# An elementwise product and GELU on one core: y's 5 KB rows loaded and computed first, its 59 KB rows loaded as 44 and 15 KB

## The chip, the cores and the metric

The kernel runs on one core of one Trainium2 chip. The metric is the device time of one execution in microseconds (us). Three runs of the kernel before took 119.72, 119.79 and 119.82 us; their median, 119.79 us, is the time before.

## The reference

x and y are float32 arrays of 1024 x 4096. The output has the same shape and type:

```python
z = x * y
return (0.5 * z * (1 + np.tanh(np.sqrt(2 / np.pi) * (z + 0.044715 * z ** 3)))).astype(np.float32)
```

So the kernel reads 2 x 16.78 MB, multiplies elementwise, applies GELU in its tanh form, and writes 16.78 MB.

## The kernel before

As the work is elementwise, the kernel takes x, y and the output as flat arrays and cuts them in three pieces (`PIECES`). Piece (a, b) is 128 x (b - a) numbers in one run of memory, seen as 128 rows, one for each partition of SBUF. In columns of 4 bytes the pieces are 0 to 1280 (rows of 5 KB, 640 KB in all), 1280 to 17664 (rows of 64 KB, 8192 KB) and 17664 to 32768 (rows of 59 KB, 7552 KB). A transfer of a piece has 128 rows, which the trace shows as 128 data packets, 8 for each of the 16 DMA engines, and 16 packets of 4 bytes that close it.

All of x has its place in SBUF (`xs`, 128 x 32768). The product and the GELU are written over x in place, and the stores read from there. y goes through a smaller buffer (`ys`, 128 x 20440), so that a part of y can be loaded only when the products that read the older part in its place are done. `Y_LOADS` lists the loads of y in order, each with its columns and its place in `ys`; `Y_FREE` says how many products must be done before each; `STEPS` cuts each load into the widths that DVE multiplies at a time; `STORES` lists the stores in order. Everything has its own semaphore (`sem_x`, `sem_y` and `sem_o` by transfer, `sem_mul` and `sem_act` as counts of products and GELUs).

The order on each engine is the order in which the code issues. There is no scheduler.

- SP issues nearly all transfers, into one queue. Its order before: x's 5 KB rows (hoisted to the start of the program, line 71), then a wait until these have landed, y's 64 KB rows (line 75), x's 59 KB rows (line 71), y's 59 KB rows after the third product, y's 5 KB rows after the fourth product. Then the stores (line 115): the 64 KB rows once the last but one load of y has landed (line 113) and their GELUs are done (line 114), the 59 KB rows and the 5 KB rows once their GELUs are done. At the end SP waits for the stores and clears the semaphores.
- ACT issues one transfer, x's 64 KB rows, hoisted to the start as well, into a queue of its own. Then it does one GELU for each product (line 106), after that product (line 105).
- DVE waits for the load of x and of y that a stretch needs (lines 94 and 95) and multiplies (line 98): four products of 4096 columns, seven of 2048 and one of 768, and one of 1280.

Of the kernel before, what the change touches and what calls it, by code (L numbers as in the profile page):

```python
# [1 line left out]

# [4 lines left out]


F32 = mybir.dt.float32
GELU = mybir.ActivationFunctionType.Gelu_apprx_tanh  # L10

PIECES = [(0, 1280), (1280, 17664), (17664, 32768)]

Y_LOADS = [(1280, 17664, 4056), (17664, 32768, 0), (0, 1280, 15104)]

Y_FREE = [0, 3, 4]

STEPS = [[4096] * 4, [2048] * 7 + [768], [1280]]  # L20
STORES = [(1280, 17664), (17664, 32768), (0, 1280)]
Y_BUF = 20440


def _hoist(nc, issued):

    here = nc.cur_bb.bb.instructions
    first = nc.main_func.blocks[0].instructions
    for ins in issued:
        del here[next(k for k, i in enumerate(here) if i is ins or i.name == ins.name)]  # L30
    engine = issued[0].engine
    at = next(
        k
        for k, i in enumerate(first)
        if i.engine == engine and type(i).__name__ == "InstDrain"
    )
    first[at:at] = issued


@with_exitstack  # L40
def kernel(
    ctx: ExitStack,
    tc: tile.TileContext,
    x: bass.AP,
    y: bass.AP,
    out: bass.AP,
):
    nc = tc.nc
    P = nc.NUM_PARTITIONS

    def columns(t, a, b):

        flat = t.flatten_outer_dims().rearrange("r c -> (r c)")
        pa, pb = next(q for q in PIECES if q[0] <= a and b <= q[1])
        return flat[P * pa : P * pb].rearrange("(p c) -> p c", p=P)[:, a - pa : b - pa]


    tc.close()
    tc.compile()  # L59

    xs = nc.alloc_sbuf_tensor("xs", [P, PIECES[-1][1]], F32).ap()
    ys = nc.alloc_sbuf_tensor("ys", [P, Y_BUF], F32).ap()
    sem_x = [nc.alloc_semaphore(f"sem_x{i}") for i in range(len(PIECES))]
    sem_y = [nc.alloc_semaphore(f"sem_y{i}") for i in range(len(Y_LOADS))]
    sem_mul = nc.alloc_semaphore("sem_mul")
    sem_act = nc.alloc_semaphore("sem_act")
    sem_o = [nc.alloc_semaphore(f"sem_o{i}") for i in range(len(STORES))]

    def load_x(i, engine=nc.sync):
        a, b = PIECES[i]  # L70
        return engine.dma_start(out=xs[:, a:b], in_=columns(x, a, b)).then_inc(sem_x[i], 16)

    def load_y(i):
        a, b, r = Y_LOADS[i]
        return nc.sync.dma_start(
            out=ys[:, r : r + b - a], in_=columns(y, a, b)
        ).then_inc(sem_y[i], 16)

    _hoist(nc, [load_x(0).ins])
    _hoist(nc, [load_x(1, nc.scalar).ins])  # L80
    nc.sync.wait_ge(sem_x[0], 16)
    load_y(0)
    load_x(2)
    for i in range(1, len(Y_LOADS)):
        if Y_FREE[i]:
            nc.sync.wait_ge(sem_mul, Y_FREE[i])
        load_y(i)

    n = 0
    done = {}  # L90
    for i, (a, b, r) in enumerate(Y_LOADS):
        for j, (xa, xb) in enumerate(PIECES):
            if xa <= a < xb:
                nc.vector.wait_ge(sem_x[j], 16)
        nc.vector.wait_ge(sem_y[i], 16)  # L95
        c = a
        for w in STEPS[i]:
            nc.vector.tensor_mul(  # L98
                out=xs[:, c : c + w],
                in0=xs[:, c : c + w],  # L100
                in1=ys[:, r + c - a : r + c - a + w],
            ).then_inc(sem_mul, 1)
            n += 1
            done[c + w] = n
            nc.scalar.wait_ge(sem_mul, n)
            nc.scalar.activation(  # L106
                out=xs[:, c : c + w], in_=xs[:, c : c + w], func=GELU
            ).then_inc(sem_act, 1)
            c += w

    for i, (a, b) in enumerate(STORES):
        if i == 0:
            nc.sync.wait_ge(sem_y[-2], 16)
        nc.sync.wait_ge(sem_act, done[b])
        nc.sync.dma_start(out=columns(out, a, b), in_=xs[:, a:b]).then_inc(sem_o[i], 16)
    for i in range(len(STORES) - 1):
        nc.sync.wait_ge(sem_o[i], 16)
    nums = sorted(s.num for s in [*sem_x, *sem_y, *sem_o[:-1], sem_mul, sem_act])
    assert nums == list(range(nums[0], nums[-1] + 1))
    nc.sync.sem_clear(range(nums[0], nums[-1] + 1))  # L120
    nc.sync.wait_ge(sem_o[-1], 16).then_inc(sem_o[-1], -16)


# [1 line left out]
_INS = ['x', 'y']  # L125
_OUTS = [((1024, 4096), 'float32')]


# [23 lines left out]
```

## Time and profile before

| what | value |
|---|---|
| median of the runs | 119.79 us |
| span of the profiled execution, first to last instruction | 118.5 us |
| its own time | not listed apart from the span; the median of the runs is 1.27 us above the span |
| bytes moved | 50.33 MB, 425 GB/s over the span |
| DVE busy | 35.2 us in 13 products |
| ACT busy | 31.0 us: 13 GELUs and the load of a table |
| y's 64 KB rows | issued at 13.57, landed at 42.56 us |
| y's 59 KB rows | issued at 55.78, landed at 78.25 us |
| y's 5 KB rows | issued at 60.1, landed at 79.8 us |
| stores | issued from 78.27 to 97.7 us, last closing packets at 118.5 us |

Means of one product and one GELU by shape, in ns: 4419 and 3616 for 4096 columns, 2285 and 1910 for 2048, 1481 and 1252 for 1280, 950 and 826 for 768.

How to read it: the span runs from the first to the last instruction of the profiled execution. "Busy" of DVE and ACT is the time in their instructions; an issue of a transfer is not counted as busy, and its data move later, on the 16 DMA engines. "Landed" is the moment when the semaphore of a transfer is complete. The chain of waits is followed back from the last instruction of the compute engines. The packet records of the trace give start, duration, size and queue of each packet, though not the DMA engine that moved it.

### The profile page before, as it was taken

How to read it: one execution, taken by the hardware profiler on the slowest of the kernel's cores; microseconds unless marked ns; L12 is line 12 of the kernel's file. 1: busy time of each engine (PE TensorE's matmuls, PEld its weight loads, DVE VectorE, ACT ScalarE, POOL GpSimd, SP SyncE). 2: the span in 40 equal slices, each digit the busy share in tenths (PEclk: the TensorE clock that was granted, in tenths of full speed). 3: DMA queues.
4: the chain of work that ended last, by engine and by line, in shares of the span. 5: the costliest groups of instructions: out<-in, count | busy, mean ns of one | idle time of the engine just before them, and what ended most of it. 6: DMA issues, size and time to landing. Idle time of an engine off the chain costs nothing.

```text
span 118.5 us, 82 instructions
## 1 busy us (share of the span) xinstructions
DVE 35.2 (30%) x13; ACT 31.0 (26%) x14; POOL 0.2 (0%) x4
## 2 busy tenths in 40 slices
DVE  0000000000000069999920000059999940000000
ACT  4000000000000000977975000006998990000000
POOL 0000000000000000000000000000000000000000
DMA  9888899889988897797797797798899887977975
GB/s 492 382 382 382 354 575 487 354 354 398 664 354 354 354 652 326 326 652 326 326 632 347 326 632 347 326 575 354 354 531 531 354 354 326 652 326 326 652 326 221
DMA packets 1296, 50.33 MB, mean 425 GB/s; under 512 B 144, under 2 KB 144, under 8 KB 528
## 3 DMA queue, kind: packets, MB, share of 16 engines
q1 hardware_dynamic: 1152, 41.94, 82.2%
q10 hardware_dynamic: 144, 8.39, 16.5%
HBM read 33.55 MB, written 16.78 MB: 425 GB/s over the span
## 4 chain that ended last, share of the span: by engine, by line
DMA 55%; DVE 24%; ACT 3%; issue 1%; DVEq 0%
DMA ys<-in_y_dram 43%; DVE xs L98 24%; DMA xs<-in_x_dram 11%; ACT xs L106 3%; DVEq L95 0%
## 5 line engine op out<-in xcount | busy, mean ns | idle before, releaser
L98 DVE TENSOR_TENSOR xs<-xs,ys 128x2048 f32<-128x2048 f32 (+3 forms) x13 | 35.2, 2777 | 60.9 <-DMA ys<-in_y_dram 60.9
L106 ACT ACTIVATE xs<-xs 128x2048 f32<-128x2048 f32 (+3 forms) x13 | 29.7, 2301 | 65.1 <-DVE xs L98 65.1
L106 ACT ACT_TABLE_LOAD x1 | 1.3, 1283 | 1.6 <-PEq L59 1.6
L136 POOL MEMSET const-bfloat16-1.0<- 128x1 bf16 x1 | 0.1, 103 | 0.0
L136 POOL MEMSET const-uint8-127<- 128x1 uint8 x1 | 0.1, 102 | 0.0
L136 POOL MEMSET const-float32-0.0<- 128x1 f32 x1 | 0.1, 100 | 0.2 <-issue 0.2
L136 POOL MEMSET const-float32-1.0<- 128x1 f32 x1 | 0.1, 99 | 0.0
## 6 DMA issues: line engine op xcount, KB each, us to landing
xs<-in_x_dram SPq DMA_DIRECT2D x1, 7552.0 KB, 46.5
ys<-in_y_dram SPq DMA_DIRECT2D x1, 7552.0 KB, 22.5
out_dram<-xs SPq DMA_DIRECT2D x1, 7552.0 KB, 20.4
xs<-in_x_dram SPq DMA_DIRECT2D x1, 640.0 KB, 13.6
ys<-in_y_dram SPq DMA_DIRECT2D x1, 640.0 KB, 19.7
out_dram<-xs SPq DMA_DIRECT2D x1, 640.0 KB, 20.8
xs<-in_x_dram ACTq DMA_DIRECT2D x1, 30.4
ys<-in_y_dram SPq DMA_DIRECT2D x1, 29.0
```

The source lines that it names most:

```text
L98: nc.vector.tensor_mul(out=xs[:, c : c + w], in0=xs[:, c : c + w], in1=ys[:, r + c - a : r + c - a + w],).then_inc(sem_mul, 1)
L106: nc.scalar.activation(out=xs[:, c : c + w], in_=xs[:, c : c + w], func=GELU).then_inc(sem_act, 1)
L136: nc = _bacc.Bacc("TRN2", target_bir_lowering=False, num_devices=1)
```

## The change

y's 5 KB rows become the first of y's loads. SP issues them directly behind the program's start, without the wait for x's 5 KB rows, and y's 64 KB rows and x's 59 KB rows behind them. The product and GELU of the 5 KB stretch come first on DVE and ACT. y's 59 KB rows are loaded as two transfers, 44 KB and 15 KB of each row: the 44 KB after the third product, the 15 KB after the fourth. As the 5 KB product now counts as the first, these are the second and third product of the 64 KB stretch. The products of the 59 KB stretch are cut accordingly: five of 2048 and one of 1024, then 2048 and 1792. There are still 13 products and 13 GELUs. The order of the stores stays; line 113 (`sem_y[-2]`), which is unchanged, now names the 44 KB load where it named the 59 KB load.

```diff
-Y_LOADS = [(1280, 17664, 4056), (17664, 32768, 0), (0, 1280, 15104)]
+Y_LOADS = [(0, 1280, 0), (1280, 17664, 4056), (17664, 28928, 0), (28928, 32768, 11264)]
 
-Y_FREE = [0, 3, 4]
+Y_FREE = [0, 0, 3, 4]
 
-STEPS = [[4096] * 4, [2048] * 7 + [768], [1280]]
+STEPS = [[1280], [4096] * 4, [2048] * 5 + [1024], [2048, 1792]]
 STORES = [(1280, 17664), (17664, 32768), (0, 1280)]
 Y_BUF = 20440
...
     _hoist(nc, [load_x(0).ins])
     _hoist(nc, [load_x(1, nc.scalar).ins])
-    nc.sync.wait_ge(sem_x[0], 16)
     load_y(0)
+    load_y(1)
     load_x(2)
-    for i in range(1, len(Y_LOADS)):
+    for i in range(2, len(Y_LOADS)):
         if Y_FREE[i]:
             nc.sync.wait_ge(sem_mul, Y_FREE[i])
         load_y(i)
```

## The prediction, made before the changed kernel was run

> **What bounds the kernel now.** I read four views, in this order: the chain of work that ended last, the busy times by stretch, the waits of the DMA queue's own engine (SP), and the DMA issues. The chain in order of time says that every long step before the tail is a load:
>
> ```profile
> 0.00 13.55 DMA xs<-in_x_dram
> ...
> 13.57 28.99 DMA ys<-in_y_dram
> ...
> 55.78 22.47 DMA ys<-in_y_dram
> ...
> 78.35 1.53 DVE xs L98
> ...
> 93.88 3.80 ACT xs L106 x3
> ```
>
> The chain stops at ACT's last GELU at 97.7 us, yet the span is 118.5 us: the last 21 us are stores, which the chain leaves out. So I go by stretches that cover it all (columns: length, DVE, ACT and POOL busy, clock, mean busy share of the 16 DMA engines, GB/s):
>
> ```profile
> 0.00:1.00 1.00, 0.00 (x0) 0.00 (x0) 0.20 (x4) 1.00 0.00 0
> 1.00:42.60 41.60, 0.00 (x0) 1.28 (x1) 0.00 (x0) 1.00 1.03 442
> 42.60:60.40 17.80, 17.43 (x4) 11.13 (x4) 0.00 (x0) 1.00 1.00 434
> 60.40:78.30 17.90, 0.00 (x0) 3.34 (x1) 0.00 (x0) 1.00 0.92 399
> 78.30:79.90 1.60, 1.55 (x1) 0.00 (x0) 0.00 (x0) 1.00 1.97 835
> 79.90:99.20 19.30, 16.22 (x9) 15.26 (x9) 0.00 (x0) 1.00 1.00 430
> 99.20:117.00 17.80, 0.00 (x0) 0.00 (x0) 0.00 (x0) 1.00 0.92 395
> 117.00:118.50 1.50, 0.00 (x0) 0.00 (x0) 0.00 (x0) 1.00 0.63 256
> ```
>
> A transfer is booked in the stretch where its packet starts, so a stretch can show more than 1 and its neighbour less (0.92 beside 1.97); together they are full. The reader is to see that no stretch between 1 us and 118 us has idle DMA engines, while DVE and ACT are idle most of the time. The packet records of the trace say it exactly: from the first packet (1.01 us) to the last (118.12 us) 16 packets run at every moment, but for 1 to 2 us (13.0 of 16, the ramp) and 79 to 80 us (14.8 of 16). The bound is the bytes: 50.33 MB through 16 busy engines. A change can win only the small holes, or lose by adding packets or opening a hole.
>
> SP's waits show which holes could be there:
>
> ```profile
> SPq L75 <- DVE xs L98: 45.4, 2, 41.4
> SPq L117 <- DMA out_dram<-xs: 18.9, 1, 18.9
> SPq L115 <- ACT xs L106: 18.7, 2, 17.9
> SPq L115 <- DMA ys<-in_y_dram: 14.5, 1, 14.5
> SPq L75 <- DMA xs<-in_x_dram: 12.0, 1, 12.0
> ```
>
> The last line is the wait that the change removes, the fourth the one that it moves to another transfer. Both are idle time of an issuing engine; each costs something only if the queue runs dry behind it.
>
> **The base.** The trace has only the span of the profiled execution, 118.5 us; the median of the runs, 119.79 us, is 1.27 us above it. Nothing in the change touches what lies around the span, so I add differences to 119.79.
>
> **Part 1: the wait for x's first piece goes, y's 5 KB rows go second in SP's queue.** The wait held SP until 13.57 us. Meanwhile x's first 64 KB piece, issued by ACT, kept all 16 engines busy (16.0 of 16 running in each microsecond from 2 to 15 us). So the wait cost nothing and its removal gains 0. The 5 KB packets of y now alternate with x's 64 KB packets as x's own 5 KB packets did. What does a pair cost? In the records from 10 to 13 us, where the two kinds alternate, every 5 KB packet takes its usual 196 ns and every 64 KB packet 2418 ns: 0 extra. From 5 to 10 us, 23 such pairs show 31.5 ns of extra time per engine in all, or 22 ns a pair (31.5 x 16 / 23). In the first round (2.3 to 5.2 us) x's 64 KB packets take 124 ns more than 2420 on the mean. Upper bound: 8 pairs per engine at 124 ns, 0.99 us; lower bound 0, as nothing in the rows makes packets shorter. I take 0, since y's 5 KB packets alternate later, where the 10 to 13 us row is nearest.
>
> **Part 2: what is then late.** All of y's 64 KB stretch comes 8 packets later, 8 x 196 ns = 1.57 us: it lands at 42.56 + 1.57 = 44.1 us. DVE's four products (4.43 us the first, 4.33 the others) end at 48.6, 53.0, 57.3 and 61.7 us. The product of the 5 KB stretch is long done by then: its 8 packets alternate with x's 64 KB ones, which end by about 23 us, so it lands near 25 us, and its 1.48 us on DVE and 1.25 us on ACT lie under y's load. SP's two later y loads wait for the third and fourth product, as before by number; with the 5 KB product counted, that is now 53.0 and 57.3 us. The queue then still holds x's last piece, until 60.41 + 1.57 - 0.42 = 61.6 us (0.42 is from the last packet's end to the landing: 77.83 and 78.25 us for y's 59 KB load). So SP has 8.6 and 4.3 us in hand, and the queue doesn't run dry. Were it late, each microsecond past 61 us would cost one.
>
> **Part 3: y's 59 KB rows as 44 and 15.** One transfer more. Packets of 5 KB take 196 ns and of 59 KB 2232 ns: 37.7 ns per KB and 7.5 ns per packet. So 44 KB takes 1666 ns, 15 KB 573 ns, together 7.5 ns over 2232. Eight rows per engine: 0.06 us; one more 4-byte closing packet, 9 ns. Sum +0.07 us. Records in one queue abut (the next starts within 4 ns), so no other cost is seen; the bounds are 0.01 us (closing packet alone) and 0.10 us (with such a 4 ns at each of the 8 packets added).
>
> The Trainium skill, "DMA: Bandwidth & Descriptors", section "Anatomy of one DMA", fits each DMA (on GpSimd's path) as about 2.0 us fixed plus its bytes; a transfer more would by that make 119.79 + 2.0 = 121.8 us, an estimate from that page. The trace has a row against it: y's 640 KB landed 1.57 us after the 59 KB load before it (79.82 and 78.25 us), exactly its packets' time, so that behind another transfer no fixed part is left.
>
> **Part 4: the first store's cover.** The first store is issued once the last but one y load has landed. Now that leaves 1.57 us of y's 5 KB packets to hide it: issue 78.27 us, its first packets 79.11 to 79.39 us. Engines that had ended earlier (from 78.9 us) stood idle, 1.2 us over 16 engines, 0.08 us on the mean; the engine that ended last (79.38 us) went on at 79.39 us without a hole. After: 44 KB land at 60.41 + 1.57 + 8 x 1.666 = 75.3 us, the store is issued then and 8 x 573 ns = 4.6 us of packets cover it. The hole closes. Gain: 0 if the last engine sets the end, 0.08 us if the engines even out. Their spread falls from 0.27 us at 79 us to 0.17 us at the end, so they do in part; I take 0.04 us.
>
> **Part 5: the end.** The 44 KB products start at 75.4 us: five of 2048 columns (2.3, then 2.2 us each) and 1024 (1.1 us, between 0.87 for 768 and 1.40 for 1280) end at 87.6 us, 2048 and 1792 at 91.8 us, ACT's last at 93.5 us. The 15 KB rows have landed at 75.3 + 4.6 = 79.9 us. So the second store is issued at 93.5 instead of 96.5 us, the last right behind it instead of at 97.7 us, both still ahead of the first store's end (98.9 us). That was covered before as well: gain 0. The last store has the same 5 KB rows: 0.
>
> **Sum:** 0 + 0.07 - 0.04 + 0 = +0.03 us, so **119.82 us**.
>
> **Rivals.** (a) *Faster: the hole at 79 us is larger without the profiler.* The last engine's first store packet comes 1.12 us after the issue (79.39 - 78.27), the others' 0.84 us and more. x's first 64 KB load needed 2.17 us (issue 0.13, first packet 2.30 us). With that the last engine would stand 1.05 us, and closing it gives 119.79 - 1.05 + 0.07 = 118.81 us. It decides where the last engine's delay is over 1.43 us (0.31 us of hole). Against it: the profile shows no hole on that engine. Chance 0.09. (b) *Slower: the opening's mixed packets hold each other up.* Place: 3 to 24 us, 8 pairs per engine. At the first round's 124 ns a pair: 119.82 + 0.99 = 120.8 us; it decides from about 26 ns a pair. For it: the first round, and 22 ns from 5 to 10 us (0.18 us, 120.0 us, just inside the bound). Against it: 0 from 10 to 13 us. Chance 0.08. (c) *The change doesn't close the hole*, because the store is held by ACT or the 15 KB rows are late: 119.79 + 0.07 = 119.86 us. ACT is done with the stretch at 65 us, ten before it is needed. It lies within the forecast's bound; its chance is in the remainder.
>
> **Numbers.** About 0.2% (0.24 us) is what a measurement of this kernel tells from no change. Within it: forecast and (c), 0.83; faster 0.09; slower 0.08. The forecast's own bounds are -0.08 + 0.01 and +0.10, so 119.72 to 119.89; the runs shown differ by 0.1 us; with 22 ns a pair it is 120.0, and toward (a) I go as far as a store whose first packets come after 1.01 us, as those of x's first load did: 0.17 us later, 119.79 - 0.17 + 0.01 = 119.63 us. With a few hundredths for the runs' spread on both sides the range is 119.60 to 120.02 us; the rest of (a) and (b), 0.17, lies outside.
>
> **What would show it.** Right: 16 engines full from 3 to 118 us; no hole near 79 us; y's 64 KB landing near 44.1 us, first store issued near 75.3 and last near 93.9 us; span within 0.15 us of 118.5. Wrong: 64 KB packets over 2440 ns in the opening (b), a span much shorter than its packets' sum allows (a), or y's later loads issued after 61 us, which would open a hole that I have not priced in.

## The result, and the profile after

The changed kernel takes **121.14 us** (median of five runs, 120.77 to 121.28) against 119.79 us before (five runs, 119.72 to 119.90): 1.0099 times the time, 95% interval 1.0088 to 1.0110. It is slower by 1.35 us, where 0.03 us was forecast. The profiled execution took 120.77 us, with a span of 119.4 us; before, the span was 118.5 us.

The chain of waits of the changed kernel, in order of time (start, length, what):

```profile
1.95 42.14 DMA ys<-in_y_dram
...
52.98 22.30 DMA ys<-in_y_dram
...
75.37 5.35 DVE xs L98 x3
...
91.77 1.70 ACT xs L106
```

Up to 75 us all went as worked out. y's 64 KB rows landed at 44.10 us (forecast 44.1), the next load was issued at 52.98 us (53.0), the 44 KB rows landed at 75.27 us (75.3). ACT ends at 93.5 us (93.5), four microseconds earlier than before, and the whole is still later. As before, the chain says nothing of the end, since it stops at ACT.

The waits of SP (us in total, times, longest) show the two that the change moved:

```profile
SPq L75 <- DVE xs L98: 54.1, 2, 50.1
SPq L117 <- DMA out_dram<-xs: 23.0, 1, 23.0
SPq L115 <- ACT xs L106: 17.8, 1, 17.8
SPq L115 <- DMA ys<-in_y_dram: 10.0, 1, 10.0
```

The wait for x is gone. The first store's wait for y (last line) is shorter, 10.0 instead of 14.5 us, as that store now needs only the 44 KB rows. But SP stands 4.1 us longer at the end, waiting for stores (line 117). The stores are issued earlier and don't end earlier.

Where the time went is in five stretches of 1 us around the turn from loads to stores (DVE, ACT and POOL busy, clock, DMA share, GB/s; a packet is booked where it starts):

```profile
76.00:77.00 1.00, 1.00 (x1) 0.00 (x0) 0.00 (x0) 1.00 1.02 430
77.00:78.00 1.00, 1.00 (x2) 0.31 (x1) 0.00 (x0) 1.00 1.05 307
78.00:79.00 1.00, 1.00 (x1) 1.00 (x1) 0.00 (x0) 1.00 1.02 215
79.00:80.00 1.00, 1.00 (x2) 0.71 (x2) 0.00 (x0) 1.00 1.33 508
80.00:81.00 1.00, 1.00 (x1) 1.00 (x1) 0.00 (x0) 1.00 1.82 786
```

The DMA share stays at 1 and the rate falls to half: 215 GB/s from 78 to 79 us. The engines are busy and move less. The packet records name the victims. Of the 128 packets of 15 KB, 48 took over 590 ns (up to 1342), the others 573 to 581; the sum above 573 is 1.02 us per engine, between 76.5 and 80.4 us. (The first expectation below says 58 packets, a miscount, and 0.98 us, which is the sum above 581 ns.) The store's first packet comes at 79.7 us, though it was issued here:

```profile
75.29 0.35 SPq L115 DMA_DIRECT2D out_dram<-xs  x1
```

From the first packet to the last the changed kernel needs 118.03 us, before 117.11 (1.01 to 118.12 us; the 118.5 us that the table before calls the last closing packets is the moment when their semaphore is complete): 0.92 us more. The slow packets (1.02), one transfer more (0.07) and the closed hole (-0.08) make 1.01 us, against these 0.92. The profiled execution is the fastest of the five; what the median has on top of it, 0.37 us, is in no trace.

### The profile page after: what moved, and what is told of

It reads as the page before. It is cut to its first block, busy times and chain, and to the rows that moved or that the text cites. A ratio compares the mean times of both kernels' runs of the same rounds, so it can differ in the third digit from the quotient of the medians.

```text
span 119.4 us, 84 instructions
## 1 busy us (share of the span) xinstructions
DVE 35.3 (30%) x13; ACT 31.1 (26%) x14; POOL 0.2 (0%) x4
## 4 chain that ended last, share of the span: by engine, by line
DMA 54%; DVE 20%; ACT 1%; issue 1%; SPq 0%; DVEq 0%
DMA ys<-in_y_dram 54%; DVE xs L98 20%; ACT xs L106 1%; SPq L75 0%; DVEq L95 0%
## 5 line engine op out<-in xcount | busy, mean ns | idle before, releaser
L98 DVE TENSOR_TENSOR xs<-xs,ys 128x2048 f32<-128x2048 f32 (+4 forms) x13 | 35.3, 2778 | 56.4 <-DMA ys<-in_y_dram 56.4
L106 ACT ACTIVATE xs<-xs 128x2048 f32<-128x2048 f32 (+4 forms) x13 | 29.8, 2302 | 60.8 <-DVE xs L98 60.8
```

The costliest lines, as they stand in the source:

```text
L98: nc.vector.tensor_mul(out=xs[:, c : c + w], in0=xs[:, c : c + w], in1=ys[:, r + c - a : r + c - a + w],).then_inc(sem_mul, 1)
L106: nc.scalar.activation(out=xs[:, c : c + w], in_=xs[:, c : c + w], func=GELU).then_inc(sem_act, 1)
```

## The experiments

Theory 1: a store that is issued long before the loads ahead of it end slows these loads at the turn. "The turn" is the stretch in which the engines go over from the last packets of the loads to the first of the store. Rivals: the 15 KB rows themselves, the products that run beside them, or the new order of the loads. Each run stands beside runs of the kernel before on the same chip, whose medians were 119.85 to 119.89 us; behind each median stand the ratio to these runs and its 95% interval.

**Only the cut of the 59 KB rows.**

```diff
-Y_LOADS = [(1280, 17664, 4056), (17664, 32768, 0), (0, 1280, 15104)]
+Y_LOADS = [(1280, 17664, 4056), (17664, 28928, 0), (28928, 32768, 11264), (0, 1280, 15104)]
-Y_FREE = [0, 3, 4]
+Y_FREE = [0, 3, 4, 0]
-STEPS = [[4096] * 4, [2048] * 7 + [768], [1280]]
+STEPS = [[4096] * 4, [2048] * 5 + [1024], [2048, 1792], [1280]]
```

> The kernel before with y's 59 KB rows loaded as 44 and 15 KB and nothing else changed: y's 5 KB rows stay the last load and cover the first store's issue for 1.57 us as before. In the changed kernel's trace 58 of the 128 packets of 15 KB took more than 590 ns (up to 1342) where 573 ns is their usual time, 0.98 us per engine in all, from 76.9 to 80.3 us, after the first store had been issued at 75.29 us behind them. Theory 1 (a store that waits in the queue behind loads slows those loads): here the store is issued only when the 15 KB rows have landed, so they run at 573 ns; time = before + one transfer more, 119.79 + 0.07 = 119.86 us. Theory 2 (the 15 KB rows are themselves slow, by how they lie in memory): they are slow here too, about 119.86 + 0.98 = 120.8 us. Theory 3 (the products and GELUs of the 44 KB stretch, which run beside the 15 KB load, slow it): also about 120.8 us.

Measured: 119.95 us, ratio 1.0009 (0.9998 to 1.0021). All 15 KB packets took 573 ns or a few more, with the same products beside them. The rows, their place in memory and the products are by themselves not the cause, and one more transfer costs about what the forecast said (0.08 us between the medians, 0.07 forecast).

**Only the order, with the store early.**

```diff
-Y_LOADS = [(0, 1280, 0), (1280, 17664, 4056), (17664, 28928, 0), (28928, 32768, 11264)]
+Y_LOADS = [(0, 1280, 0), (1280, 17664, 4056), (17664, 32768, 0)]
-Y_FREE = [0, 0, 3, 4]
+Y_FREE = [0, 0, 4]
-STEPS = [[1280], [4096] * 4, [2048] * 5 + [1024], [2048, 1792]]
+STEPS = [[1280], [4096] * 4, [2048] * 7 + [768]]
```

> The changed kernel with y's 59 KB rows in one load again; y's 5 KB rows stay first. The wait of the first store for the last but one load of y is then met at 44 us, so the first store is issued when its GELUs are done, near 65.3 us, and waits in the queue behind x's and y's 59 KB rows until 79.9 us. Theory 1: the store slows the 59 KB packets in the queue ahead of it: at least the one loss of about 1.0 us that the changed kernel shows (120.8 us), up to a third of the 14 us that remain (0.98 us lost of 2.9 us in the changed kernel), 124 us. Theories 2 and 3: no 15 KB rows and no products beside y's last load, no loss; no hole before the store: 119.79 - 0.04 = 119.75 us.

Measured: 121.26 us, 1.0121 (1.0106 to 1.0137). The store is issued at 65.50 us. The 59 KB packets up to 76.7 us are at 2232 ns; only the last on each engine is slow, 16 packets of up to 3.54 us, 1.09 us per engine. So the loss belongs to the turn and not to the 14 us in which the store stood in the queue. On top there is half a microsecond of idle engines at 99 us, since the late products delay the second store.

**Only the order, with the store late**, and **the changed kernel with the store late.** Both have this edit, the first on top of the edit just shown:

```diff
-            nc.sync.wait_ge(sem_y[-2], 16)
+            nc.sync.wait_ge(sem_y[-1], 16)
```

> The same as the run before it, but the first store waits for y's last load. No theory has slow packets here (nothing is queued behind loads, no 15 KB rows, no products beside loads). All expect a hole of 0.42 us (last packet to landing) plus 0.84 to 1.12 us (issue to first packet) ahead of the store, less what the engines' spread of 0.5 us takes: about 1.3 us, 121.1 us. It measures the price of a hole, and whether the removal of the wait for x's first piece and the new order cost anything beyond it.

> The changed kernel, with its 44 and 15 KB loads, but the first store waits for the 15 KB load, the last one. Theory 1: the 15 KB packets run at 573 ns, as no store waits behind them; a hole of about 1.3 us takes its place: 119.86 + 1.3 = 121.2 us. Theories 2 and 3: the 15 KB packets are slow as in the changed kernel (0.98 us), and the hole comes on top: 122.1 us.

Measured: 121.44 us (1.0117 to 1.0145) and 121.53 us (1.0125 to 1.0153). No packet of the last loads is slow in either, and the 15 KB ones took 573 to 581 ns. The hole is there instead. With the order alone y's last load landed at 79.81 us, before at 79.82: up to here the order and the missing wait for x cost nothing. Then:

```profile
78.00:79.00 1.00, 0.00 (x0) 0.00 (x0) 0.00 (x0) 1.00 0.00 0
79.00:80.00 1.00, 0.10 (x1) 0.00 (x0) 0.00 (x0) 1.00 0.01 0
80.00:81.00 1.00, 1.00 (x1) 0.00 (x0) 0.00 (x0) 1.00 2.46 1049
```

The last packets of 59 KB started before 78 us and end at 79.0 us on the mean; nothing but closing packets starts until 80.66 us. The hole is 1.7 us on the mean of the engines, and its price 1.57 and 1.66 us (over 119.87) where about 1.3 was expected, because I took the engines' spread off a sum that runs from the last packet of all (79.37 us). The mean engine had ended 0.33 us before that, so the spread adds to its hole.

**The cut at 54 and 5 KB**, with the changed kernel's order (here and in the next cuts only the lines that replace the changed kernel's are shown):

```diff
+Y_LOADS = [(0, 1280, 0), (1280, 17664, 4056), (17664, 31488, 0), (31488, 32768, 13824)]
+Y_FREE = [0, 0, 4, 4]
+STEPS = [[1280], [4096] * 4, [2048] * 6 + [1536], [1280]]
```

> The changed kernel with y's 59 KB rows cut as 54 and 5 KB instead of 44 and 15, so that the first store, issued when the 54 KB rows have landed, has 8 packets of 196 ns (1.57 us) of loads ahead of it, as in the kernel before; order of the loads as in the changed kernel. Theory 1 (a store queued behind loads costs about 1.0 us once it is there while each engine still has some 2 to 3 us of loads to do; both runs with an early store lost 1.0 to 1.1 us whatever the lead, 5 or 14 us): the store's packets come to the engines about 1 us after its issue, as the loads end, so no packet is slow and the hole is 0.08 us as before: 119.8 to 119.9 us. Rival, the new order of the loads is itself what costs: about 120.8 us or more, since the order is the changed kernel's.

Measured: 120.00 us, 1.0011 (1.0003 to 1.0020). The order is not the cause. The profiled execution is the slowest of its eleven (120.33 us); its hole at the turn is 0.2 us, and 0.15 us of slow packets lie before the store was issued. **The same with the store early:**

```diff
-            nc.sync.wait_ge(sem_y[-2], 16)
+            nc.sync.wait_ge(sem_y[1], 16)
```

> The run before it, but the first store waits for y's 64 KB load (landed at 44 us) instead of the 54 KB load, so that it is issued when its GELUs are done, near 65.4 us, and stands in the queue behind the 54 and 5 KB rows. Theory 1: the loss of 1.0 us is there again, in the last packets of the loads, 120.8 to 120.9 us; nothing but the moment of the issue differs from the run before it. Rival, it is the kind of rows at the end (15 KB, 59 KB) that was slow and not the store behind them: as the run before it, 119.8 us.

Measured: 121.10 us, 1.0106 (1.0091 to 1.0122). Only the moment of the issue differs, 65.26 instead of 78.75 us, and 1.07 us per engine is lost, nearly all in packets of 5 KB (up to 606 ns instead of 196). These are SP's issues of the stores (start of the first, us to the end of the third), first with the 54 and 5 KB cut alone, then with the early store:

```profile
78.75 19.52 SPq L115 DMA_DIRECT2D out_dram<-xs  x3
```

```profile
65.26 31.86 SPq L115 DMA_DIRECT2D out_dram<-xs  x3
```

**The cut at 49 and 10 KB, and at 47 and 12 KB.**

```diff
+Y_LOADS = [(0, 1280, 0), (1280, 17664, 4056), (17664, 30208, 0), (30208, 32768, 12544)]
+Y_FREE = [0, 0, 4, 4]
+STEPS = [[1280], [4096] * 4, [2048] * 5 + [2304], [2048, 512]]
...
+Y_LOADS = [(0, 1280, 0), (1280, 17664, 4056), (17664, 29696, 0), (29696, 32768, 12032)]
+Y_FREE = [0, 0, 3, 4]
+STEPS = [[1280], [4096] * 4, [2048] * 5 + [1792], [2048, 1024]]
```

> The changed kernel with y's 59 KB rows cut as 49 and 10 KB: 8 packets of about 385 ns, 3.1 us of loads, lie between the store's issue and its turn. Theory 1 with a threshold (all or nothing): the loss of 1.0 us if 3.1 us are beyond it, 120.8 us. Theory 1 with a loss that grows with the overlap of store and loads (issue to first packet takes about 1 us, so 0.5 us of overlap with the 5 KB cut, 2 us here, 3.5 us with 15 KB): about half the loss, 120.3 us.

> The changed kernel with 47 and 12 KB instead of 44 and 15: 8 packets of about 460 ns, 3.7 us of loads, lie ahead of the store at its issue, between the 3.1 us that cost nothing and the 4.6 us that cost 1.0 us. A threshold gives either 119.9 to 120.0 or 120.8 to 121.2 us; a loss that grows with the lead beyond 3.1 us gives about 40% of it, 120.3 us.

Measured: 119.97 us, 1.0008 (0.9999 to 1.0017), with no slow packet and no hole; and 120.55 us, 1.0054 (1.0041 to 1.0068), with 0.3 us of slow packets in the profiled execution, the fastest of its runs (120.14 to 120.78 us). The first speaks against a loss that grows with every overlap of store and loads (120.3 us), and fits a threshold above its lead (3.1 us of packets for each engine, 2.61 us by the table below, which counts from the issue). The second lies between the two forms that I wrote for it (120.3 us for a loss that grows beyond there; 120.0 at most or 120.8 us and more for all or nothing), so the form stays open; the loss begins between the two cuts.

**The first store in ACT's queue.** SP issues only the other two; ACT's part is

```diff
+        if i == 1:
+            a, b = STORES[0]
+            nc.scalar.wait_ge(sem_y[-2], 16)
+            nc.scalar.wait_ge(sem_act, done[b])
+            nc.scalar.dma_start(out=columns(out, a, b), in_=xs[:, a:b]).then_inc(sem_o[0], 16)
```

> The changed kernel with the first store issued by ACT, into ACT's queue, at the same moment (the 44 KB rows landed, near 75.3 us), so that it goes beside the 15 KB loads and not behind them. The engines take turns between the two queues, so the 15 KB rows land some 15 us later, and the whole is slower by a hole before the second store (several us); what counts are the packets. Theory 1a (loads and stores in flight together slow each other): 15 KB packets well over 573 ns or 64 KB store packets well over 2420 ns for as long as they alternate. Theory 1b (it is the turn from loads to stores within one queue): 15 KB packets at 573 ns and store packets at 2420 ns.

Measured (one run): 121.19 us. Neither form came out as written, since the store's packets did not go beside the loads. It was issued at 75.39 us, and its first packet is recorded at 79.91 us, when nearly all 15 KB rows were done. Those were as slow as in the changed kernel (up to 1462 ns, 1.1 us per engine), at a time when no store packet was recorded:

```profile
77.00:78.00 1.00, 1.00 (x2) 0.21 (x1) 0.00 (x0) 1.00 1.10 276
78.00:79.00 1.00, 1.00 (x1) 1.00 (x1) 0.00 (x0) 1.00 0.97 215
```

So, by this one run, the loss doesn't need one queue for both. What the engines do in that time the records don't show.

**The changed kernel with its store 2.4 us later.**

```diff
-            nc.sync.wait_ge(sem_y[-2], 16)
+            nc.sync.wait_ge(sem_mul, 6)
```

> The changed kernel, with one wait exchanged: the first store waits for the sixth product (the first of the 44 KB stretch, done near 77.65 us) instead of the landing of the 44 KB rows (75.3 us). So it is issued 2.3 us later, with about 2.2 us of the 15 KB loads still ahead of it. All loads, rows and products are the changed kernel's. Theory 1 (the early store is the cause; 3.1 us of loads ahead of it cost nothing with the 10 KB cut, 4.6 us cost 1.0 us): all 15 KB packets at 573 to 580 ns, no hole, 119.79 + 0.07 = 119.86 us to 120.0 us. Rival, the 15 KB rows or the work beside them bring the loss once a store is anywhere behind them: 120.8 us or more.

Measured: 119.96 us, 1.0007 (0.9999 to 1.0016). One wait gives back nearly all: 1.18 us between the medians. The same stretches as for the changed kernel, and the issue:

```profile
77.00:78.00 1.00, 1.00 (x2) 0.27 (x1) 0.00 (x0) 1.00 1.05 445
78.00:79.00 1.00, 1.00 (x1) 1.00 (x1) 0.00 (x0) 1.00 1.40 600
79.00:80.00 1.00, 1.00 (x2) 0.71 (x2) 0.00 (x0) 1.00 1.82 786
```

```profile
77.73 0.35 SPq L115 DMA_DIRECT2D out_dram<-xs  x1
```

DVE and ACT do nearly the same work in them as in the changed kernel; only the rate differs (600 for 215 GB/s). The store is issued later and lands earlier: 77.73 + 21.5 = 99.2 us against 75.29 + 24.8 = 100.1 us, by these rows of the DMA issues (KB where listed, us to landing), the changed kernel first:

```profile
ys<-in_y_dram SPq DMA_DIRECT2D x1, 1920.0 KB, 23.4
...
out_dram<-xs SPq DMA_DIRECT2D x1, 24.8
```

```profile
ys<-in_y_dram SPq DMA_DIRECT2D x1, 1920.0 KB, 22.5
...
out_dram<-xs SPq DMA_DIRECT2D x1, 21.5
```

**A small store amid the loads**, added to the run before:

```diff
     load_x(2)
+    nc.sync.wait_ge(sem_act, 1)
+    a, b = STORES[2]
+    nc.sync.dma_start(out=columns(out, a, b), in_=xs[:, a:b]).then_inc(sem_o[2], 16)
...
-    for i, (a, b) in enumerate(STORES):
+    for i, (a, b) in enumerate(STORES[:2]):
```

> The run with the store that waits for the sixth product, and in addition the 5 KB store no longer last but in SP's queue between x's 59 KB load and y's 44 KB load, issued when its GELUs are done (near 27.7 us), 34 us before its turn near 61.6 us. If each early store costs a fixed loss of about 1.0 us where the queue turns from loads to stores, whatever its size: +1.0 us on the run with the gated store, 120.9 us, with slow packets in x's last 59 KB row near 60 us. If the loss grows with the bytes of the store that stands behind the loads (0.6 MB here, 8.4 MB there): near 0, 119.9 us.

Measured: 121.70 us, 1.0160 (1.0147 to 1.0173). x's last 59 KB packets take up to 3.62 us, 1.34 us per engine. Expected was about 120.9 us. Against the run before it the first-to-last packet time is 1.42 us longer in the profiled execution and the median 1.74 us; what the median has on top is in no trace. A store of 0.6 MB costs at least as much as one of 8.4 MB: the loss goes with the turn and not with the store's bytes.

**The kernel before without its wait.**

```diff
-        if i == 0:
-            nc.sync.wait_ge(sem_y[-2], 16)
```

> The kernel before without the first store's wait for the last but one load of y (lines 112 and 113); the store is then issued when its GELUs are done, near 63.8 us, 15 us ahead of its turn, and stands behind y's 59 KB and 5 KB rows. Nothing of the change is in it. Theory 1 (a store that is issued more than some 3 to 4 us ahead of the end of the loads costs about 1.0 to 1.3 us at the turn, whatever else the kernel does): 120.8 to 121.2 us, with slow packets among y's 5 KB rows and none earlier. If the loss needs something of the changed kernel (order of the loads, rows cut in two): 119.7 to 119.9 us, as an early store closes the hole of 0.08 us.

Measured: 121.16 us, 1.0111 (1.0095 to 1.0128), with nothing of the change in it. Slow are y's 5 KB packets and the last of 59 KB (up to 3.05 us; I expected none before the 5 KB rows), 1.36 us per engine:

```profile
78.00:79.00 1.00, 0.28 (x1) 0.00 (x0) 0.00 (x0) 1.00 0.97 210
79.00:80.00 1.00, 1.00 (x1) 0.00 (x0) 0.00 (x0) 1.00 0.87 246
```

The runs in order of the lead, the time from the first store's issue to the end of the last load packet (the small store amid the loads, with two turns from loads to stores, is left out):

| kernel | lead, us | slow packets, us per engine | median, us |
|---|---|---|---|
| changed, store late | -0.46 | 0.00, but a hole of 1.6 | 121.53 |
| order, store late | -0.45 | 0.00, but a hole of 1.7 | 121.44 |
| before | 1.11 | 0.00 | 119.79 |
| only the cut | 1.13 | 0.00 | 119.95 |
| 54 and 5 KB | 1.17 | 0.01 | 120.00 |
| changed, store 2.4 us later | 1.73 | 0.02 | 119.96 |
| 49 and 10 KB | 2.61 | 0.02 | 119.97 |
| 47 and 12 KB | 3.28 | 0.28 | 120.55 |
| **changed** | 5.07 | 1.02 | 121.14 |
| changed, store from ACT | 5.41 | 1.1 | 121.19 (one run) |
| order, store early | 15.0 | 1.09 | 121.26 |
| 54 and 5 KB, store early | 15.2 | 1.07 | 121.10 |
| before, store early | 17.1 | 1.36 | 121.16 |

Free were the leads from 1.1 to 2.6 us. At -0.45 us the queue ran dry, and from 3.3 us up the loads slowed down; nothing between -0.45 and 1.1 us was run.

## Why the prediction was wrong, point by point

- **Parts 1, 2 and 3 held.** The removed wait and the new order cost and gained nothing (79.81 for 79.82 us at the end of the loads). In the opening the 64 KB and 5 KB packets did not hold each other up: from 2 to 24.5 us their time above 2418 and 196 ns is 0.13 us per engine, before 0.18. So rival (b) has the right sign and the wrong place, and that its 0.99 us is near the loss is chance. The later loads were issued with time in hand. One transfer more is within a tenth of a microsecond.
- **Part 4 failed.** "The hole closes. Gain: 0 if the last engine sets the end, 0.08 us if the engines even out": the hole did close, but I priced an earlier issue as a cover that can only help. 4.6 us of packets ahead of the store are not a better cover than 1.57; they lengthen the lead from 1.11 to 5.07 us, and that costs 1.02 us in the profiled execution. The term was put at -0.04 us and came to +0.94 (1.02 lost, 0.08 gained).
- **What misled me.** "Records in one queue abut (the next starts within 4 ns), so no other cost is seen" was read from loads behind loads and stores behind stores. The only turn from loads to stores in the trace of before had a lead that is free, 1.11 us. The range took its upper end from the opening alone. The wait on line 113, for which SP is idle 14.5 us (the fourth of the prediction's lines on SP's waits, booked at the issue in line 115), was the row to ask about: what would happen if that store came earlier? I asked only what would happen if it came later. The signs of being right could not tell either: the landing at 44.1 us, the closed hole, the issues at 75.3 and 93.9 us and the full engines all came true, and only the span (119.4 us) was off.
- **Part 5 held** in its times (ACT's last at 93.5 us) and in its gain, 0.
- The rule "Overlap DMA with compute" of the Trainium skill ("DMA: Bandwidth & Descriptors", section "Rules for kernel authors") advises to issue a transfer early, as its fixed cost is then hidden. For these stores the runs differ: early was 1.1 to 1.3 us dearer in three pairs of runs that differ by one wait (54 and 5 KB, the changed kernel, the kernel before).

What stays open: why the engines run at a lower rate, down to half, in those 2 to 3 us, although no store packet is recorded yet; whether the limit of the lead (between 2.6 and 3.3 us) is a time or a number of bytes ahead; and the 0.37 us by which the changed kernel's median exceeds its profiled execution. The 47 and 12 KB runs scatter by 0.64 us, which may be a loss that differs between executions, but that is not shown: the runs with only the cut, whose trace has no loss, scatter by 0.71 us.

## What to carry to other kernels

In a kernel that keeps the DMA engines full, a busy share of 1 doesn't say that they are at full rate: look at GB/s and at the packets' durations around each turn from loads to stores. Issue the first store behind a run of loads neither after their end nor as early as it could be, here 1.1 to 2.6 us before the last load packet ends, and use a wait on something that happens at that time (a product will do). A wait of an issuing engine that looks idle may be holding this distance, so before moving it, price both directions. The limits of the lead were measured on this kernel alone.

## What the runs showed of the hardware that I had not expected

- A store waiting behind loads slows the last of these loads: 215 GB/s from 78 to 79 us in the changed kernel, where 430 were moved from 76 to 77 us; 1.0 to 1.4 us are lost for a lead of 5 us and more.
- The loss is about the same for a store of 0.6 MB (1.34 us) and of 8.4 MB (1.02 to 1.36 us), for rows of 5, 15 and 59 KB ahead of it, and for a store from ACT's queue (1.1 us, one run).
- From issue to first packet the store took 0.84 us where the engines were free (79.82 to 80.66 us). With the landing before it, a store that waits for the last load leaves the engines idle for 1.6 to 1.7 us on the mean.
